# A limit of four on loaded rows of x, and a precedence of 0.1 on TensorE for the state streams, in a hybrid GLA and RWKV-7 step

## The chip, the cores and the metric

The kernel runs on one core of a Trainium2 chip. The metric is the device time of one execution in microseconds (us), as the median of several runs; lower is better. The profile is that of one execution.

## The reference, cut to what matters

One layer is computed for 1024 new tokens (the prompt) and 8 single tokens with a stored state each (the samples). All arithmetic is float32.

```python
p = x @ w_in                                  # (1024 + 8) x 1024 by 1024 x 9360 columns
p_gla, p_rwkv, p_gate = split(p)
o_gla, S_gla   = gated_linear_attention(p_gla)  # 4 heads, in chunks, silu-gated
o_rwkv, S_rwkv = rwkv7_scan(p_rwkv)             # 16 heads, one state of 64 x 64 each, silu-gated
m   = sigmoid(gate_a) * (o_gla @ w_up_gla) + sigmoid(gate_b) * (o_rwkv @ w_up_rwkv)
out = layernorm(2 ** 0.25 * x + m @ w_out)
# also returned: the final states S_gla and S_rwkv, and the last projected row, of prompt and samples
```

## The kernel before

**Tiling.** Everything is kept transposed: a row is a tile of 128 channels (partitions) by tokens. The tokens go in two passes (`PASS`, line 29): pass 0 has 512 prompt tokens and the 8 samples, in two column tiles of 260; pass 1 has the other 512 prompt tokens in one tile of 512. In each pass the 73 column groups of `w_in` are projected one after the other. One such projection is a block (`blocks`, line 670): for k from 0 to 7 three matmuls, `hi*xh`, `hi*xl` and `lo*xh`, since each float32 operand is split in a high and a low part. After both passes come the up-projections (of `o_gla`, then `o_rwkv`, pass 0, then pass 1) and the output projection (of `mg`, pass 0, then pass 1), also as blocks.

**The change of x.** Whenever the block stream goes on to another input, `load_x` (line 583) brings the eight row tiles of the new one: a DMA into a buffer of the pool `row` (`raws`), a copy on ScalarE into `xh{k}` (`high`, line 594; the finished ones stand in `his`), and a subtraction into `xl{k}` (`low`, line 602), which then frees the raw row. `xh{k}` and `xl{k}` exist once; they come free when the last block of the old input has done its step k (line 700). `load_x` is started three blocks ahead of that (`AHEAD`). There are eight changes: x of pass 0, x of pass 1, `o_gla` and `o_rwkv` of pass 0 and of pass 1, `mg` of pass 0 and of pass 1. For the two of x, `low_rank` (line 714) also multiplies the raw rows, in groups of three rows (0 to 2, 3 to 5, 6 and 7), into one PSUM bank of `big` for each column tile, and a raw row isn't freed before that.

**Buffers.** `row` has 26 buffers of 128 x 520 in SBUF. A block takes one row for its result before its first matmul, and, in both passes, only if another one is left over beside what is already waited for (`KEEP`, lines 268, 745, 1008, 1352). The eight PSUM banks are `proj` 2, `big` 3, `pch` 1, `pY` 2. `big` serves nearly all but the projections and the chain: the heads of GLA, `front`, `back`, `turn` and `norm` of the RWKV pairs.

**The streams.** For each of the 8 pairs of RWKV heads `pair` (line 1012) runs `front`, `back`, `turn`, `chain` and `norm`; `gla_head` (line 752) runs the four GLA heads, and in pass 0 `gla_sample` (line 886) after each of them, with eight rows held until line 863. At the end of a chain of pass 1, `state` (line 1219) takes a bank of `big`, transposes the final state `Sp` into it on TensorE, waits for the one buffer `sto`, copies, and frees the bank. `rwkv_sample` (line 1249) and `tails` (line 963) begin with transposes of the same sort; they run in one stream of the same kind, "state", from the second front of pass 1 on.

**The order.** All streams are Python generators, and a planner (`run`, line 357) puts their instructions in one order when the program is made. At each step it takes the operation with the smallest key: the start time that it estimates less a precedence, `ON_PE` for TensorE and `PRIO` for the others (line 365). Blocks have 0.0 on TensorE. A matmul with other array tiles than the one before counts as 0.09 later (`SWITCH`, lines 64 and 324); a transpose of `Sp`, 128 x 64, has other tiles than a block's 128 x 128. At equal keys the stream that stands first in the list wins. A stream that waits for a buffer offers no operation. Each engine then executes its instructions in exactly that order, and SyncE issues all DMAs in one queue in that order.

Of the kernel before, what the change touches and what calls it, by code (L numbers as in the profile page):

```python
# [55 lines left out]

KEEP = 1
AHEAD = 3
SPARE_ROWS = 8


# [12 lines left out]
PRIO = {"evacuate": 0.7, "pair": 0.4, "turn": 0.5, "chain": 0.5, "norm": 0.1, "x": 0.7, "lora": 0.2, "rank": -0.3,  # L74
        "head": 0.3, "gate": 0.05, "w": 0.3, "out": -0.1, "state": 0, "block": 0.0}
ON_PE = {"evacuate": 0.0, "pair": 0.15, "turn": 0.1, "chain": 0.15, "norm": 0.15, "x": 0.0, "lora": 0.15, "rank": 0.1,
         "head": 0.1, "gate": 0.06, "w": 0.0, "out": -0.03, "state": 0.0, "block": 0.0}

URGENT = 0.6
SIGMOID, EXP = "sigmoid_and_others", "natural_log_exp_and_others"  # L80
# [321 lines left out]
class Kern(Order):  # L402
# [180 lines left out]
    def load_x(self, src, i, wait=None, low_rank=False):  # L583

        if wait is not None:
            yield wait
        base, n = PASS[i][:2]
        raws, his, xs, used = [], [], [], [NK]
        self.xq.append(xs)
        if low_rank:  # L590
            used = [0]
            self.spawn(self.low_rank(self.ctx[i], raws, used), "rank")

        def high():
            for k in range(NK):
                yield lambda: len(raws) > k
                h = yield from self.get(f"xh{k}")
                yield self.A.copy(h[:, :n], raws[k])
                his.append(h[:, :n])

        def low():
            for k in range(NK):
                yield lambda: len(his) > k
                lo = yield from self.get(f"xl{k}")
                yield self.E.tensor_sub(lo[:, :n], raws[k], his[k].bitcast(F32))
                yield lambda: used[0] > k
                self.free(raws[k])
                xs.append((his[k], lo[:, :n]))
        self.spawn(high(), "x")
        self.spawn(low(), "x")  # L610
        for k in range(NK):
            raw = yield from self.row(n)
            rows = slice(k * P, (k + 1) * P)
            yield from self.load(f"x{k}", self.S.dma_start(
                raw, src[k] if isinstance(src, list) else src[rows, base:base + n]))
            raws.append(raw)
# [752 lines left out]
    def load_gates(self):  # L1369

        yield lambda: self.ctx[1].fronts == NPAIR and self.ctx[1].gated == NPAIR + 2 * GH
        for c in self.ctx:
            for n in range(2):
                for x in range(NK):
                    gt = yield from self.row(c.n, SPARE_ROWS)
                    yield self.S.dma_start(gt, self.sg[c.i][n][x])
                    m = None
                    if n:
                        m = yield from self.row(c.n, SPARE_ROWS)
                        yield lambda: c.half > x  # L1380
# [132 lines left out]
    def swap(self, src, i, wait=None, low_rank=False):  # L1513

        if self.plan:
            self.plan[-1].last = True
        self.todo = (max(0, len(self.plan) - AHEAD), (src, i, wait, low_rank))

# [135 lines left out]
```

## Time and profile before

| | us |
|---|---|
| median of 3 runs | 1686.61 (1685.98 to 1691.09) |
| the profiled execution | 1687.94 |
| its span, first to last instruction | 1686.2 |
| TensorE busy with matmuls in the span | 1628.7 |
| VectorE busy | 1184.6 |
| ScalarE busy | 830.7 |

Matmuls overlap, so a busy TensorE is one that has some matmul in it, at whatever clock. The granted clock is given as a share of 2.4 GHz; 0.50 is the lower of its two levels, 1.2 GHz. The page shows the span in 40 slices of 42 us, the windows show chosen stretches, the timeline single instructions with the idle time ahead of them and what ended it.

### The profile page before, as it was taken

The numbers are of one execution on the slowest core, as the hardware profiler recorded it, in microseconds if no ns is written. First come the engines' busy times: TensorE is split into PE (matmuls) and PEld (weight loads), VectorE is DVE, ScalarE is ACT, GpSimd is POOL, SyncE is SP. The second block draws the span as 40 slices with busy tenths as digits, with TensorE's granted clock in tenths as the row PEclk, the third lists the DMA queues.
The fourth block names the chain that finished last, engine by engine and source line by source line (L and its number), as shares of the span: only waits on it lengthen the run. The fifth ranks groups of instructions, "written<-read, shape, count | busy, mean of one in ns | idle before, by whom it ended". The sixth has DMA issues, their size and how long they took to land.

```text
span 1686.2 us, 29927 instructions
## 1 busy us (share of the span) xinstructions
PE 1628.7 (97%) x10322; PEld 1430.9 (85%) x10322; DVE 1184.6 (70%) x3114; ACT 830.7 (49%) x1974; POOL 86.0 (5%) x183
## 2 busy tenths in 40 slices
PE   8999999999999998999999999999989999999998
PEld 7899999999999996888878778778867889988786
DVE  6777876887688766757656477898728876656565
ACT  5456755664657465443634254526243656644210
POOL 1100000100000000000000000200000000000000
PEclk9999999999999999899999999999988999999999
DMA  9777675777587657545364625454642487788522
GB/s 291 246 228 231 217 215 152 227 246 218 160 245 228 216 158 237 170 119 174 101 206 123 186 73 176 152 163 156 202 145 67 114 275 221 236 278 278 182 78 87
DMA packets 311778, 315.26 MB, mean 187 GB/s; under 512 B 75347, under 2 KB 197084, under 8 KB 311628
## 3 DMA queue, kind: packets, MB, share of 16 engines
q1 hardware_dynamic: 311628, 313.36, 59.9%
q8 instruction: 82, 1.34, 0.3%
q14 instruction: 68, 0.56, 0.1%
HBM read 195.45 MB, written 117.82 MB: 186 GB/s over the span
## 4 chain that ended last, share of the span: by engine, by line
PE 73%; DVE 12%; DMA 7%; ACT 3%; issue 2%; SPq 2%; POOL 0%; POOLq 0%; DVEq 0%; ACTq 0%
PE proj L214 41%; PE big L214 21%; PE pY L214 7%; DVE row L214 4%; PE pch L214 4%; DMA wide<-LD 2%; SPq L214 2%; DVE X L214 2%; DVE Xt L214 2%; ACT row L214 1%; DVE wide L214 1%; DMA row<-state_rwkv 1%; DVE wlo L214 1%; DVE az L214 1%; DMA wraw<-w_up_gla 1%
## 5 line engine op out<-in xcount | busy, mean ns | idle before, releaser
L214 PE MATMUL proj<-xl,whi 128*128 128x260 f32 (+1 forms) x1928 | 637.5, 331 | 0.0
L214 PE MATMUL proj<-xh,whi 128*128 128x260 f32 (+1 forms) x1928 | 635.9, 330 | 0.0
L214 PE MATMUL proj<-xh,wlo 128*128 128x260 f32 (+1 forms) x1928 | 635.0, 329 | 0.0
L214 PEld LDWEIGHTS proj<-xh,wlo 128*128 128x128 f32 x1928 | 364.9, 189 | 29.9 <-issue 6.6
L214 PEld LDWEIGHTS proj<-xh,whi 128*128 128x128 f32 x1928 | 365.2, 189 | 28.5 <-issue 5.4
L214 PEld LDWEIGHTS proj<-xl,whi 128*128 128x128 f32 x1928 | 364.9, 189 | 28.6 <-issue 6.5
L214 DVE TENSOR_TENSOR row<-row 128x256 f32<-128x256 f32 (+6 forms) x326 | 161.7, 503 | 23.8 <-ACT row L214 11.8
L214 ACT CAST whi<-wraw 128x512 fp32r<-128x512 f32 x210 | 129.9, 622 | 95.7 <-PE proj L214 51.7
L214 DVE TENSOR_TENSOR wlo<-wraw,whi 128x512 fp32r<-128x512 f32 x205 | 141.0, 691 | 40.5 <-ACT whi L214 37.3
L214 ACT ACTIVATE row<-row 128x512 f32<-128x512 f32 (+4 forms) x229 | 138.4, 611 | 44.6 <-DVE row L214 26.3
L214 DVE TENSOR_TENSOR Xt<-X,wide 128x60 f32<-128x60 f32 (+24 forms) x496 | 105.4, 212 | 43.8 <-DMA wide<-LD 31.2
L214 ACT ACTIVATE row<-proj,omu 128x260 f32<-128x260 f32 (+1 forms) x99 | 54.1, 547 | 150.2 <-PE proj L214 149.9
L214 PE MATMUL big<-row 128*128 128x64 f32 (+4 forms) x712 | 115.6, 282 | 12.5 <-DVE row L214 11.5
L214 PEld LDWEIGHTS big<-row 128*128 128x128 f32 (+1 forms) x712 | 96.9, 193 | 23.3 <-DVE row L214 13.5
L214 ACT ACTIVATE s0p<-wide,pc 64x64 f32<-64x64 f32 x256 | 88.1, 344 | 52.7 <-DVE wide L214 48.5
L214 DVE TENSOR_TENSOR X<-X,Xt 128x60 f32<-128x60 f32 (+24 forms) x496 | 104.8, 211 | 11.9
L214 ACT COPY wide<-pch 64x64 f32<-64x64 f32 x221 | 45.5, 206 | 114.3 <-PE pch L214 110.4
L214 DVE SCALAR_TENSOR_TENSOR row<-proj,pv,row 128x259 f32<-128x259 f32 (+1 forms) x99 | 56.3, 569 | 49.7 <-ACT tail L214 33.7
L214 DVE SCALAR_TENSOR_TENSOR wide<-pch,pc,s0p 64x64 f32<-64x64 f32 x224 | 63.1, 282 | 38.3 <-PE pch L214 33.7
L214 POOL TENSOR_TENSOR row<-row 128x512 f32<-128x512 f32 (+7 forms) x43 | 45.5, 1059 | 794.4 <-ACT row L214 211.7
L214 ACT COPY row<-big 128x128 f32<-128x128 f32 (+7 forms) x165 | 46.7, 307 | 66.8 <-PE big L214 63.5
L381 ACT ACT_TABLE_LOAD x56 | 71.8, 1283 | 1.0
(254 smaller groups left out, 2560.6 us busy)
## 6 DMA issues: line engine op xcount, KB each, us to landing
wraw<-w_in SPq DMA_DIRECT2D x146, 256.0 KB
wh<-whi SPq DMA_DIRECT2D x146, 256.0 KB
wl<-wlo SPq DMA_DIRECT2D x146, 256.0 KB
whi<-wh SPq DMA_DIRECT2D x146, 256.0 KB
wlo<-wl SPq DMA_DIRECT2D x146, 256.0 KB
wide<-LD SPq DMA_DIRECT2D x64, 128.0 KB
wraw<-w_up_gla SPq DMA_DIRECT2D x32, 256.0 KB
wraw<-w_up_rwkv SPq DMA_DIRECT2D x32, 256.0 KB
```

Of the source, the lines that this page charges most:

```text
L214: ways.append((eng, lambda call=call: call(out, *args, **kw), price(eng, name, out, args, ins)))
L381: self.nc.scalar.preload_act_table_set(self.table)
```

## The change

Ahead of each raw row, `load_x` now waits until fewer than four rows are loaded and not yet copied into `xh`. The first change of x of the program is exempt: there `low_rank` is true and the pass, `i`, is 0. Streams of the kind "state" get the precedence 0.1 on TensorE in place of 0.0; on the other engines theirs stays 0.

```diff
+RAWS = 4
...
 ON_PE = {"evacuate": 0.0, "pair": 0.15, "turn": 0.1, "chain": 0.15, "norm": 0.15, "x": 0.0, "lora": 0.15, "rank": 0.1,
-         "head": 0.1, "gate": 0.06, "w": 0.0, "out": -0.03, "state": 0.0, "block": 0.0}
+         "head": 0.1, "gate": 0.06, "w": 0.0, "out": -0.03, "state": 0.1, "block": 0.0}
...
         self.spawn(high(), "x")
         self.spawn(low(), "x")
         for k in range(NK):
+            yield lambda: k - len(his) < RAWS or low_rank and not i
             raw = yield from self.row(n)
```

## Rows read from the trace of the kernel before

**Rows 1.** The page: busy time of the engines; granted clock by slices
```profile
PE 1628.7 (97%) x10322; PEld 1430.9 (85%) x10322; DVE 1184.6 (70%) x3114; ACT 830.7 (49%) x1974; POOL 86.0 (5%) x183
...
PEclk9999999999999999899999999999988999999999
```
**Rows 2.** Windows, long ones: from:to, length, TensorE busy (matmuls), clock, DMA share, GB/s
```profile
50.00:650.00 600.00, 590.39 (x4649) 1.00 0.69 213
700.00:1350.00 650.00, 627.60 (x3256) 0.98 0.48 145
1350.00:1686.00 336.00, 323.07 (x1860) 1.00 0.64 204
```
**Rows 3.** Windows of the stretches with a lower clock, same columns
```profile
672.00:680.00 8.00, 2.72 (x12) 0.54 0.47 160
680.00:688.00 8.00, 7.67 (x42) 0.61 0.10 35
960.00:996.00 36.00, 30.78 (x151) 0.86 0.26 76
1236.00:1280.00 44.00, 35.90 (x154) 0.77 0.20 62
```
**Rows 4.** Timeline of TensorE: start, us, instruction, idle before it and releaser
```profile
670.32 0.28 PE L214 MATMUL proj<-xl,whi 128*128 128x260 f32 x1
670.44 0.28 PE L214 MATMUL proj<-xh,wlo 128*128 128x260 f32 x1
676.22 1.02 PE L214 MATMUL big<-row 128*128 128x8 f32 x4 [5.49 <-DVE row L214]
...
680.68 1.02 PE L214 MATMUL big<-row 128*128 128x8 f32 x4 [0.33 <-DVE row L214]
681.56 0.57 PE L214 MATMUL proj<-xh,whi 128*128 128x260 f32 x1
```
**Rows 5.** Timeline of the DMA queue, first and last loads of x for pass 1 (eight in all)
```profile
646.30 1.43 SPq L214 DMA_DIRECT2D row<-xT  x2
...
654.82 0.65 SPq L214 DMA_DIRECT2D row<-xT  x1
```
**Rows 6.** Timeline of ScalarE, x of pass 1 is copied
```profile
693.41 4.27 ACT L214 CAST xh<-row 128x512 fp32r<-128x512 f32 x8
```
**Rows 7.** Timeline of VectorE, last writes of final states in chains of pass 1
```profile
846.60 0.60 DVE L214 SCALAR_TENSOR_TENSOR Sp<-pch,pc,s0p 64x64 f32<-64x64 f32 x2 [2.25 <-PE pch L214]
...
933.16 0.58 DVE L214 SCALAR_TENSOR_TENSOR Sp<-pch,pc,s0p 64x64 f32<-64x64 f32 x2
...
1018.51 0.58 DVE L214 SCALAR_TENSOR_TENSOR Sp<-pch,pc,s0p 64x64 f32<-64x64 f32 x2
...
1085.50 0.60 DVE L214 SCALAR_TENSOR_TENSOR Sp<-pch,pc,s0p 64x64 f32<-64x64 f32 x2 [0.19 <-PE pch L214]
...
1185.54 0.60 DVE L214 SCALAR_TENSOR_TENSOR Sp<-pch,pc,s0p 64x64 f32<-64x64 f32 x2 [0.31 <-PE pch L214]
```
**Rows 8.** Timeline of TensorE, transposes of final states and what follows them
```profile
962.32 0.27 PE L214 MATMUL big<-cons,smp 128*128 128x128 f32 x1
962.42 0.38 PE L214 MATMUL big<-cons,Sp 128*64 128x128 f32 x2
963.32 2.00 PE L214 MATMUL big<-X,gg 128*128 128x64 f32 x16 [0.52 <-ACT sto L214]
...
1237.96 0.49 PE L214 MATMUL big<-cons,Sp 128*64 128x128 f32 x3
```
**Rows 9.** The chain of work that ended last: a load of 256 KB, issue to use
```profile
671.00 3.68 DMA row<-vd
```
**Rows 10.** Timeline of VectorE, low parts of x for pass 1
```profile
694.07 4.90 DVE L214 TENSOR_TENSOR xl<-row,xh 128x512 fp32r<-128x512 f32 x8 [0.22 <-ACT xh L214]
```
**Rows 11.** Waits of TensorE after 1340 us: total, times, longest
```profile
PE big L214 <- DVE wlo L214: 1.0, 1, 1.0
PE pY L214 <- DVE xl L214: 0.6, 1, 0.6
```

## The prediction

> **What bounds the kernel now.** I read the page first. TensorE has matmuls in it for 97% of the span and its clock is full in all but three slices [rows 1]: the kernel is bound by TensorE, and only what empties it or slows its clock can be won. Second, the windows. From 50 to 650 us, nearly all of pass 0, 590.39 of 600 us are busy at a clock of 1.00, so 1.6% are idle; from 1350 us to the end it is as dense but for the last microseconds [rows 2]. From 700 to 1350 us, pass 1, busy time times clock is 627.60 x 0.98 = 615 of 650 us; at the 1.6% of pass 0 it would be 640. So about 25 us are lost in pass 1, beside what lies just ahead of it. Third, shorter windows around the low digits of the clock, which find three places: 672 to 688, 960 to 996 and 1236 to 1280 us [rows 3]. Busy time alone hides a part of them, since a matmul at 1.2 GHz is busy for twice as long; length less busy time times clock is the loss.
>
> Place A: 8 - 2.72 x 0.54 = 6.5 us and 8 - 7.67 x 0.61 = 3.3 us, and the idle time from 670.7 to 672, 1.3 us: 11.1 us. Place B: 36 - 30.78 x 0.86 = 9.5 us. Place C: 44 - 35.90 x 0.77 = 16.4 us [rows 3, 4]. Together 37.0 us, of which B and C are 25.9, the same as the 25 of the long window. Each value holds to about 1 us, as clock and busy share are means.
>
> **Why these places are there.** At A the timeline shows projections up to 670.44, then only the four groups of tiny products of `gla_sample`, the first after 5.49 us of waiting, and the next projection at 681.56, right behind the last of them [rows 4]. The projection has all its operands from pass 0; what it lacks can only be the row for its result. A count along the code at that point (no row of the trace shows the pool): GLA head 3 holds 8 rows, pair 7 holds 3, pair 6 in `norm` 3, gates 4, and x of pass 1 holds 8, since its loads are issued from 646.30 to 655.5 while the copies come only at 693.41 [rows 5, 6]. That is 26 of 26. The next rows to come free are those of head 3, behind its last tiny product, which is where the projection goes on.
>
> At B and C no x is loaded. There the banks of `big` run out. The final states of the first five pairs of pass 1 are written at 846.60, 933.16, 1018.51, 1085.50 and 1185.54 [rows 7]; their transposes, which hold a bank each from then on, run at 962.42 (two) and 1237.96 (three), 116, 29, 219, 152 and 52 us later [rows 7, 8]. In both cases the transposes stand directly ahead of the bubble, not after a wait for data. From the code: a block and a state both have 0.0, blocks always have a matmul ready, and a transpose of `Sp` pays 0.09 for the change of tiles, so the state never wins until the blocks stop. So from 933 to 962 us and from 1185 to 1238 us all three banks are taken (before 962 the third by the transpose of `smp`, which goes with the others [rows 8]), heads, fronts and norms stand still with their rows in hand, the rows run out, the blocks stop, and only then do the states go. Then the held-up work comes as one chain without projections between its links, which is the bubble.
>
> **The change, part by part.** *The limit.* It leaves four rows of x unloaded until `xh` comes free, so 22 of 26 rows are taken at A. The gate's temporary and the next block's row fit, and the two blocks left in pass 0 run there. A's 11.1 us go. The clock's part goes with it, since no pause is left to lower it. What is late next is the change of x itself, some 11 us earlier.
>
> What the limit adds is a wait at each of seven changes (the first is exempt): rows 4 to 7 are issued once a copy of rows 0 to 3 is emitted, and so behind more of the DMA queue, among the weight loads and the stores of gates; the queue holds nothing back by it, for the wait is in the planner and no instruction of SyncE waits for a copy. TensorE's bound from below is nothing, or a little less than nothing (four loads fewer compete with the weights): what hides the load is the rest of the old input's last block, 7 steps, and the new one's first four. Matmuls of 260 columns start 0.12 us apart [rows 4], so a step of three takes 0.36 us and 11 steps 3.9 us; with 512 columns they take longer. The bound from above is a whole load, copy and subtraction: 3.68 us [rows 9], 4.27/8 = 0.5 us [rows 6] and 4.90/8 = 0.6 us [rows 10], 4.8 us for each change, 33.6 us for seven. The values now, with all rows there, are waits of 1.0 and 0.6 us near such changes [rows 11]. I take 0.7 us each, by these rows and by 3.9 of 4.8 us being covered: 5 us in all. The low-rank products of the last five rows of x move behind the copies; their sum stays, and they fill the wait there. Their bank is held from the start of the load to the change as before.
>
> Against holding loads back there is a rule. The Trainium skill, "Trainium Kernel Development and Optimization", section Best Practices, tells to double-buffer so that DMA overlaps compute. By it each late load would show whole, which is the rival "late x" below; the trace has it both ways, as the early rows are what takes the buffers at A.
>
> *The precedence.* With 0.1 a state transpose has a key of +0.09 - 0.1 = -0.01 against a block, and wins; the one of `smp` wins by 0.1. No instruction is added; eight transposes of `Sp` and a few others, 0.1 us from start to start [rows 8], change places. Waits that they bring: at most the copy and the store behind one `sto`, and the states are 67 us or more apart [rows 7]. The bank comes back within a few us, B and C have three banks, as pass 0 has, and pass 0 has no such bubble. B and C give 25.9 us; at pass 0's 1.6%, the 60 us of dense work that stays in A, B and C keeps 1.0 us idle. `rwkv_sample` starts about 100 us earlier and holds its three to five rows earlier; between 996 and 1236 us it held them with no loss of that size, so I cost it at nothing, and at one more place like A, 11 us, if that cover is gone.
>
> *Sum.* 37.0 - 1.0 - 5 = 31 us. The profiled execution took 1687.9 us, 1.3 us over the median of the runs; 1686.6 - 31 = 1655.6, so 1656 us. Nothing behind pass 1 takes the gain back: the last chains would be done earlier too, as they wait for banks in C, and from 1350 us on TensorE is full [rows 2].
>
> **The rivals.** *Only A (0.17).* The margin of 0.01 lies inside estimates: other streams change the tiles too, a state's start may be estimated 0.01 later, and then the second part doesn't do what it says; or rows, not banks, are what B and C lack. For it: rows were short at A with a bank free. Against: the transposes start each bubble. Time: 1686.6 - 11.1 + 5 = 1680.5, without the late loads 1675.5.
>
> *Only B and C (0.08).* The blocks stop near 670 us for want of something else, or the stop moves a block further: 1686.6 - 24.9 + 5 = 1667.
>
> *Late x (0.07), slower.* Every change shows the whole load, 33.6 us, and TensorE stands long enough that its clock falls as at A, where the 8 us behind the pause lost 3.3 us [rows 3], 23.1 us in all. With the 36 us gained at A, B and C this is 1686.6 + 56.7 - 36 = 1707. It decides from 36/7 = 5.1 us a change, against a bound of 4.8 without the clock. Against: the cover of 3.9 us or more just worked out.
>
> *Nothing moves (0.04).* All bubbles return elsewhere, since another buffer is short: 1687.
>
> **How the numbers follow.** Forecast 0.64, 1656 us, its own range 1646 (late loads cost nothing, 36 us gained, and some 4 us of the other 10 us lost in pass 1 besides) to 1667 (one new place like A). The range takes in "only A" as well: 1645 to 1682. Left out are late x, nothing moves and a tail of the forecast, under 0.2. Bound for "the same": 0.3%, about what a measurement tells, 5 us, so 1681.5 to 1691.7. Faster: 0.64 + 0.08 + most of only A, 0.13, is 0.85; the same: 0.04 + 0.04 = 0.08; slower: 0.07.
>
> **What would show it.** Right: no stretch of projections ends without another near 670 us; loads of x for pass 1 come in two lots, the second with the copies; each transpose of `Sp` starts within some 5 us of its last write, the first near 840 us, and not two or three in a row; the clock is full throughout pass 1; busy time times clock from 700 to 1300 us is at 98% or more. Wrong: transposes of `Sp` still in groups (then only A); a wait for `xl` or `xh` of over 2 us at most changes of x (then late x); a bubble with tiny products and no projections elsewhere, say where the sample's step takes its rows.

## The result, and the profile after

| | before | after |
|---|---|---|
| median of the runs, us | 1687.66 (1685.98 to 1691.09, 4 runs) | 1659.75 (1656.93 to 1662.12, 4 runs) |
| the profiled execution, us | 1687.94 | 1659.17 |
| its span, us | 1686.2 | 1657.4 |

The ratio is 0.983, 95% interval 0.981 to 0.985: 28 us less, where 31 were forecast, and 1659.75 us where 1656 stood.

The page of the changed kernel: busy times, and the granted clock in its 40 slices.

```profile
PE 1618.6 (98%) x10322; PEld 1420.0 (86%) x10322; DVE 1181.6 (71%) x3106; ACT 836.6 (50%) x1986; POOL 82.2 (5%) x179
...
PEclk9999999999999999999999999999999999999999
```

As many matmuls as before [rows 1], 10 us less of busy time, and no slice with a low clock. Windows (from:to, length, TensorE, its weight loads, VectorE, ScalarE, GpSimd, clock, DMA share, GB/s):

```profile
672.00:680.00 8.00, 7.85 (x59) 6.65 (x58) 7.31 (x26) 5.22 (x10) 1.36 (x1) 1.00 0.83 271
680.00:688.00 8.00, 8.00 (x35) 3.87 (x35) 7.00 (x20) 3.56 (x8) 0.00 (x0) 1.00 0.89 291
700.00:1300.00 600.00, 590.73 (x3166) 488.23 (x3165) 430.12 (x1216) 280.40 (x687) 32.02 (x66) 1.00 0.50 152
1350.00:1656.00 306.00, 296.94 (x1702) 257.63 (x1700) 181.04 (x345) 112.22 (x219) 2.77 (x3) 0.99 0.62 198
```

Place A, with 2.72 and 7.67 us busy at half the clock before [rows 3], is full. Pass 1 is busy for 98.5% at full clock, just over the 98% named as the sign, and as dense as pass 0 was [rows 2]; B and C are gone. Next the loads of x for pass 1 in the DMA queue (start, us), and the copies of x and of `o_gla` on ScalarE:

```profile
647.40 1.46 SPq L216 DMA_DIRECT2D row<-xT  x2
652.15 0.96 SPq L216 DMA_DIRECT2D row<-xT  x2
...
676.33 4.47 SPq L216 DMA_DIRECT2D row<-xT  x4
```
```profile
678.42 1.66 ACT L216 CAST xh<-row 128x512 fp32r<-128x512 f32 x3 [0.45 <-PE proj L216]
...
1335.51 1.68 ACT L216 CAST xh<-row 128x520 fp32r<-128x520 f32 x3
1337.61 0.62 ACT L216 CAST xh<-row 128x520 fp32r<-128x520 f32 x1
1341.71 0.62 ACT L216 CAST xh<-row 128x520 fp32r<-128x520 f32 x1 [0.86 <-DMA row<-o_gla]
```

Two lots in place of one [rows 5], and the copy of x comes 15.0 us earlier than at 693.41 [rows 6]. The copies of `o_gla` now wait for their second lot; that is the late x of the forecast. The transposes of final states on TensorE (start, us; first three and last of `Sp`, and one of `smp`):

```profile
832.77 0.27 PE L216 MATMUL big<-cons,smp 128*128 128x128 f32 x1
...
839.59 0.27 PE L216 MATMUL big<-cons,Sp 128*64 128x128 f32 x1
...
926.70 0.30 PE L216 MATMUL big<-cons,Sp 128*64 128x128 f32 x1
...
1004.19 0.27 PE L216 MATMUL big<-cons,Sp 128*64 128x128 f32 x1
...
1426.75 0.27 PE L216 MATMUL big<-cons,Sp 128*64 128x128 f32 x1
```

Each of the eight runs alone, 0.7 to 1.0 us behind the last write of its state (838.64, 926.05, 1003.24 and so on to 1425.87 us), where before a bank stayed taken for up to 219 us [rows 7, 8].

**Where the time came from.** The first copies of x of pass 1 and of `o_gla` of pass 0 cut the span in three:

| stretch, us | before | after | less by |
|---|---|---|---|
| start to the copy of x of pass 1 | 693.4 | 678.4 | 15.0 |
| from there to the copy of `o_gla` (pass 1) | 671.5 | 657.1 | 14.4 |
| from there to the end | 321.3 | 321.9 | -0.6 |

The stretches don't hold quite the same work. The groups of matmuls by form show what crossed the cuts. Ten low-rank products, 12 tiny products of `gla_sample` and 4 of 260 columns moved from the first stretch to the second. The ten, and what one pair of them takes up to the next projection, 0.96 us:

```profile
L216 PE MATMUL big<-row,wa x10: 592/598/603, 679.0 to 688.2; 128*16 128x512 f32 x10
```
```profile
682.89 1.03 PE L216 MATMUL big<-row,wa 128*16 128x512 f32 x2
683.85 0.50 PE L216 MATMUL proj<-xh,wlo 128*128 128x512 f32 x1
```

That is 10 x 0.48 + 12 x 0.09 + 4 x 0.13 = 6.4 us. From the third stretch to the second came 4 products of 512 columns (0.46 us each), 14 of 128 (0.11) and three transposes, 3.7 us. Like for like the second stretch gained 14.4 + 6.4 + 3.7 = 24.5 us, and the third lost 0.6 + 3.7 = 4.3.

Most of what the third stretch loses lies at the change to `o_gla` of pass 0. A load in the chain that ended last (start, then us from issue to use), and a window of TensorE (busy, clock, DMA share, GB/s):

```profile
1339.21 6.04 DMA row<-o_gla
```
```profile
1335.00:1350.00 15.00, 12.05 (x60) 0.89 1.03 296
```

The last late rows take 6.04 us, where the forecast took 3.68 [rows 9]. TensorE waits five times for `xh` and `xl` (2.9 us in all, the longest 1.18), and from 1346 to 1348 us it has the lower clock. That makes 15 - 12.05 x 0.89 = 4.3 us of loss; before, the 15 us from 1364 on, at the same change, lost 15 - 13.99 = 1.0 us at full clock.

### The profile page after: what moved, and what is told of

Read it like the earlier page. It is cut to its first block, busy times and chain, and to the rows that moved or that the text cites. A ratio compares the mean times of both kernels' runs of the same rounds, so it can differ in the third digit from the quotient of the medians.

```text
span 1657.4 us, 29919 instructions
## 1 busy us (share of the span) xinstructions
PE 1618.6 (98%) x10322; PEld 1420.0 (86%) x10322; DVE 1181.6 (71%) x3106; ACT 836.6 (50%) x1986; POOL 82.2 (5%) x179
## 4 chain that ended last, share of the span: by engine, by line
PE 74%; DVE 13%; DMA 6%; SPq 3%; ACT 2%; issue 2%; POOL 0%; POOLq 0%; DVEq 0%; ACTq 0%
PE proj L216 39%; PE big L216 23%; PE pY L216 7%; DVE row L216 4%; PE pch L216 4%; SPq L216 3%; DMA wide<-LD 3%; DVE X L216 2%; DVE Xt L216 2%; DVE wide L216 2%; ACT row L216 1%; DVE wlo L216 1%; DVE pair L216 1%; DMA row<-o_gla 1%; DMA LD<-gg 1%
## 5 line engine op out<-in xcount | busy, mean ns | idle before, releaser
L216 PE MATMUL proj<-xl,whi 128*128 128x260 f32 (+1 forms) x1880 | 620.9, 330 | 0.0
L216 PE MATMUL proj<-xh,whi 128*128 128x260 f32 (+1 forms) x1880 | 618.6, 329 | 0.0
L216 PE MATMUL proj<-xh,wlo 128*128 128x260 f32 (+1 forms) x1880 | 617.8, 329 | 0.0
L216 PEld LDWEIGHTS proj<-xh,wlo 128*128 128x128 f32 x1880 | 355.0, 189 | 29.0 <-issue 6.5
L216 PEld LDWEIGHTS proj<-xh,whi 128*128 128x128 f32 x1880 | 355.3, 189 | 26.3 <-issue 4.8
L216 PEld LDWEIGHTS proj<-xl,whi 128*128 128x128 f32 x1880 | 355.1, 189 | 25.9 <-issue 4.9
L216 DVE TENSOR_TENSOR row<-row 128x512 f32<-128x512 f32 (+8 forms) x333 | 162.1, 495 | 18.5 <-ACT row L216 7.9
L216 ACT COPY wide<-pch 64x64 f32<-64x64 f32 x224 | 46.2, 206 | 102.3 <-PE pch L216 98.6
L216 POOL TENSOR_TENSOR row<-row 128x512 f32<-128x512 f32 (+5 forms) x36 | 39.5, 1098 | 763.6 <-ACT row L216 347.4
L216 ACT COPY row<-big 128x128 f32<-128x128 f32 (+8 forms) x165 | 46.8, 307 | 52.3 <-PE big L216 47.2
```

The source lines that it names most:

```text
L216: ways.append((eng, lambda call=call: call(out, *args, **kw), price(eng, name, out, args, ins)))
```

## The experiments

Times are medians; the kernel before had 1687 us beside each group (1686.99, 1687.28 and 1687.61). Stretches are cut as in the table above.

**One part alone.** The limit without the precedence:

```diff
-         "head": 0.1, "gate": 0.06, "w": 0.0, "out": -0.03, "state": 0.1, "block": 0.0}
+         "head": 0.1, "gate": 0.06, "w": 0.0, "out": -0.03, "state": 0.0, "block": 0.0}
```

> The limit without the precedence. Theory: place A is a shortage of rows, B and C one of banks, and the two parts of the change act apart. A's 11 us go, B and C stay: 1687 - 11 = 1676 us (1673 to 1680). The trace should show the clock full from 668 to 690 us, x of pass 1 copied near 680 us, and transposes of Sp in groups of two and three with a bubble behind each, some 12 us earlier than before. Rival, rows are what lacks at B and C too and the limit relieves them: the whole gain, 1660 us, with no bubble in pass 1.

1680.64 us (1674.79 to 1685.27, ten runs), ratio 0.996, 0.995 to 0.998: a gain of 6 us, 0.6 us outside what I gave. Windows of A and of the old places B and C, 10 us earlier (here and below: TensorE busy, clock, DMA share, GB/s), and the transposes of `Sp`:

```profile
672.00:680.00 8.00, 7.89 (x62) 1.00 0.86 270
680.00:688.00 8.00, 8.00 (x35) 1.00 0.88 306
950.00:986.00 36.00, 30.77 (x157) 0.91 0.31 98
1226.00:1270.00 44.00, 35.82 (x161) 0.81 0.19 62
```
```profile
953.42 0.38 PE L216 MATMUL big<-cons,Sp 128*64 128x128 f32 x2
...
1227.57 0.49 PE L216 MATMUL big<-cons,Sp 128*64 128x128 f32 x3
```

A is full. B and C still lose 36 - 30.77 x 0.91 = 8.0 and 44 - 35.82 x 0.81 = 15.0 us (9.5 and 16.4 before), behind a group of two and one of three as in [rows 8]. The limit doesn't relieve them, so this rival falls. The run doesn't tell whether rows lack there for another reason, since no x is loaded at B and C; the two experiments on margin and holding below decide that.

The precedence without the limit:

```diff
-            yield lambda: k - len(his) < RAWS or low_rank and not i
```

> The precedence without the limit. Theory: B and C go, A stays with its pause of 5.5 us, its tiny products alone from 676 to 681 us and its low clock: 1687 - (29 - 11) = 1669 us (1665 to 1672). Rival, the bubbles of pass 1 are set off by the pause at A, which puts the streams out of step: then they stay, 1680 us or more. Rival, B and C are worth the 25.9 us that length less busy time times clock gave: 1661 us.

1668.29 us (1667.4 to 1670.57), ratio 0.989, 0.986 to 0.992. The same windows, and one more between them:

```profile
672.00:680.00 8.00, 2.29 (x10) 0.68 0.52 172
680.00:688.00 8.00, 7.67 (x46) 0.68 0.10 35
880.00:890.00 10.00, 7.72 (x25) 0.66 0.52 162
950.00:986.00 36.00, 35.14 (x230) 1.00 0.49 145
1226.00:1270.00 44.00, 41.84 (x221) 1.00 0.48 142
```

A stands as before, B and C are gone. So the two parts act nearly apart: by the medians they gain 6 and 19 us, 25 of the 28 us of both. From 880 to 890 us 10 - 7.72 x 0.66 = 4.9 us are lost behind one wait of 2.51 us for `l2p`, an operand of `front`; with them pass 1 would have gained 15.0 + 3.7 + 4.9 = 23.6 us like for like, nearly the 24.5 of the change.

**Margin or holding.** The precedence at 0.08, under the 0.09 of a change of array tiles:

```diff
-         "head": 0.1, "gate": 0.06, "w": 0.0, "out": -0.03, "state": 0.1, "block": 0.0}
+         "head": 0.1, "gate": 0.06, "w": 0.0, "out": -0.03, "state": 0.08, "block": 0.0}
```

> The change with a precedence of 0.08 in place of 0.1, just under the 0.09 that a change of array tiles costs. Theory: the margin decides, a transpose of Sp still loses to blocks that are ready, but one of smp, with the tiles of a block, wins and gives its bank back. Then banks are short later than before and stay so: transposes of Sp more than 20 us after their last write, again with bubbles, 1665 to 1677 us. Rival, any precedence does, since other streams change the tiles often enough: each transpose within 5 us of its last write, 1660 us.

1674.89 us (1669.62 to 1676.06). Those of `smp` run at 831.42 and 833.08, as early as in the change; those of `Sp` wait in twos again, the first of each pair over 100 us (last writes at 837.28, 923.66, 1014.35 and 1083.54):

```profile
958.14 0.38 PE L216 MATMUL big<-cons,Sp 128*64 128x128 f32 x2
...
1124.03 0.41 PE L216 MATMUL big<-cons,Sp 128*64 128x128 f32 x2
```

Around these two pairs TensorE loses 36 - 28.98 x 0.95 = 8.5 us from 955 us on and 40 - 36.22 x 0.91 = 7.0 us from 1120 us on. In these traces pass 1 takes 674.6 us, like the 674.3 of the limit alone, whose trace is its fastest run; by the medians 0.08 gains 6 of the 21 us between the limit alone and the change. The 0.01 that the forecast stood on is real, and carries most of the second part.

Then the other way round: the precedence stays, but a state takes its bank, and so runs, only when all fronts of pass 1 have begun.

```diff
     def state(self, p, S):
+        yield lambda: self.ctx[1].fronts == NPAIR
         pt = yield from self.bank("big", [C, P])
```

> The change, with each state stream made to wait, before it takes its bank, until all eight fronts of pass 1 have begun; the transposes then come in one group near 1320 us. Theory: a held bank is the cause of B and C, not a transpose that comes late, so nothing is lost: 1660 us (1657 to 1663). Rival, it is the early transposes that help, by what waits for their results: the losses of B and C come back, 1672 to 1680 us.

1663.63 us (1659.07 to 1666.94), ratio 0.986, 0.982 to 0.989: 0.6 us over what the theory gave, far below the rival. The trace separates them too: six transposes run from 1320.43 to 1326.19 us, and pass 1 loses nothing (656.1 us against 657.1):

```profile
1320.43 0.27 PE L216 MATMUL big<-cons,Sp 128*64 128x128 f32 x1
...
1326.19 0.30 PE L216 MATMUL big<-cons,Sp 128*64 128x128 f32 x1 [0.31 <-ACT sto L216]
1342.26 0.30 PE L216 MATMUL big<-cons,Sp 128*64 128x128 f32 x1 [1.36 <-ACT sto L216]
```

Nobody waits for an early transpose; what hurt was the bank taken long before it. The late ones queue behind the one `sto`, and the last stretch has 323.2 us in place of 321.9, a difference too small to be read.

**What the limit costs, and where.** The limit at the change to x of pass 1 alone:

```diff
-            yield lambda: k - len(his) < RAWS or low_rank and not i
+            yield lambda: k - len(his) < RAWS or not (low_rank and i)
```

> The change, with the limit only at the change to x of pass 1, so that the six later changes load all eight rows ahead as before. Theory: the limit costs a few us there, at most the 4 to 5 us that the stretch behind pass 1 lost beside what it was relieved of: that stretch, from the first copy of o_gla to the end, falls from 321.9 us to 317 to 320 us, the start and pass 1 stay as in the change (678 and 657 us), 1656 to 1659 us in all. Rival, late x costs nothing and the loss there has another cause: 1660 us, with 321 to 323 us in that stretch. Rival, the early rows fill the pool again at the change to o_gla and hold blocks up: over 1663 us.

1666.95 us (1662.29 to 1667.48), ratio 0.987, 0.985 to 0.990. Start and pass 1 are as in the change (678.4 and 658.2), but the last stretch takes 328.9 us, 7 more: my theory had the wrong sign, and the third rival has the time. Two parts of it take 4.9 us more each, from the first copy of `o_gla` to that of `o_rwkv` (68.9 against 64.0) and from `mg` of pass 0 to `mg` of pass 1 (60.3 against 55.4); the parts between give 2.6 back. The first loss, in the DMA queue, on TensorE and in a window:

```profile
1376.36 4.22 SPq L216 DMA_DIRECT2D row<-o_rwkv  x8
```
```profile
1378.81 2.00 PE L216 MATMUL big<-X,gg 128*128 128x64 f32 x16 [1.73 <-DVE X L216]
...
1389.76 0.79 PE L216 MATMUL pch<-wide,gg 128*128 128x128 f32 x2 [2.00 <-ACT wide L216]
```
```profile
1376.00:1394.00 18.00, 13.74 (x74) 0.66 0.80 246
```

The eight rows of `o_rwkv` are loaded while the last pair of pass 1 still runs, and its chain goes nearly without blocks at half the clock: the picture of A, 18 - 13.74 x 0.66 = 8.9 us. That the pool is empty there is argued from A, not seen, and early rows alone don't bring this loss: with the precedence alone the eight are loaded from 1385.10 us on, also while the last pair runs, and from 1350 to 1411 us TensorE is busy for 58.19 of 61 us at full clock. What else it takes stays open. The second loss is at the change to `mg`, where the kernel before had it too (its DMA queue and TensorE first, then the queue of the change):

```profile
1577.90 3.77 SPq L214 DMA_DIRECT2D row<-mg  x8
...
1583.27 0.37 SPq L214 DMA_DIRECT2D row<-w_out  x1
```
```profile
1587.80 0.49 PE L214 MATMUL proj<-whi,xh 128*128 128x512 f32 x1 [2.25 <-ACT whi L214]
```
```profile
1547.04 0.43 SPq L216 DMA_DIRECT2D row<-w_out  x1
1551.64 1.89 SPq L216 DMA_DIRECT2D row<-mg  x4
```

The last load of `w_out`, which also takes a row, stood behind eight loads of `mg`, and TensorE waited 2.25 us for its copy (2.99 in this experiment). With the limit it goes ahead of the rows for pass 1.

Two rows (`RAWS = 2` in place of 4), three (3), five (5), six (6) and seven (7):

> The change with two rows in place of four. Theory: what hides a late load is the work of the steps before it; rows 2 to 7 now come two by two, each pair a load, a copy and a subtraction (4.8 us) behind the one before, 14 us for the last, against a cover of 4 us with 260 columns and some 8 with 512: 6 to 10 us of waiting at each of seven changes where it shows in full, less where other matmuls fill it. I expect waits for xl and xh of over 2 us at most changes and 1675 to 1710 us. Rival, other streams fill all of it, so that a late load costs nothing here: 1660 us.

> The change with three rows in place of four. The last rows now come one load, copy and subtraction (4.8 us) later than with four, less what the steps hide: 2 to 5 us more at most changes, 1668 to 1690 us, between the 1660 us of four rows and the 1710 us of two. Rival, the cover is used up only below three: 1660 us.

> The change with five rows in place of four. By the count 23 of 26 rows are taken at A, which is enough: x of pass 1 copied at 678 to 681 us. Late rows are three in place of four, so no more waiting for them: 1656 to 1662 us. Rival, as with six rows: a place at the change to o_gla, where the late rows were issued 5 us behind the first copy, and bubbles in pass 1: 1668 us or more.

> The change with six rows in place of four. By the count 24 of 26 rows are taken at A: one block gets its row, the second of the two left does not. The pause comes one block later, and is shorter: copies from 682 to 689 us, 1661 to 1667 us. Rival, two free rows are enough, as one block gives its row back before the next wants one: near 679 us, 1660 us. Rival, the same as seven rows: 690 us or later.

> The change with seven rows in place of four. Theory by the count of the pool: 18 rows are held beside those of x, so 25 of 26 are taken, a block wants one and another left over, and place A comes back whole: x of pass 1 copied from 690 to 694 us, TensorE at a low clock from 672 to 688 us, 1667 to 1672 us. Rival, one row is all that the blocks lacked: copied near 679 us, 1660 us.

All, with four (as measured first) and with no limit (the precedence alone):

| rows | time, us | copy of x of pass 1 | pass 1 | first copy of `o_gla` to that of `o_rwkv` | rest |
|---|---|---|---|---|---|
| 2 | 1709.88 | 675.4 | 663.2 | 84.3 | 280.7 |
| 3 | 1681.60 | 678.4 | 665.9 | 78.9 | 255.2 |
| 4 | 1659.75 | 678.4 | 657.1 | 64.0 | 257.9 |
| 5 | 1655.39 | 679.5 | 656.8 | 63.0 | 255.5 |
| 6 (one run) | 1679.91 | 689.0 | 664.6 | 67.8 | 256.7 |
| 7 (one run) | 1672.89 | 692.7 | 656.8 | 63.8 | 257.8 |
| none | 1668.29 | 693.2 | 656.5 | 61.2 | 257.9 |

The copy of x bears out the count of the pool row by row: up to 23 of 26 taken A is gone, with 24 it stands one block later (projections run to 676.6 us in place of 670.4), with 25 it is whole. The times came out less well: five rows are 0.6 us below the range that I gave, seven 0.9 us above it and six 13 us above it, the last two by one run each. At the other end late x costs what its rival feared: with two rows the kernel is slower than before, ratio 1.014, 1.011 to 1.016, and TensorE waits 16.6 + 12.0 + 1.9 us for `xh` behind 1300 us:

```profile
PE pY L216 <- ACT xh L216: 16.6, 7, 8.1
PE big L216 <- ACT xh L216: 12.0, 5, 6.6
...
PE proj L216 <- ACT xh L216: 1.9, 3, 0.9
```

A round of load and copy there took 11.8, 5.1 and 4.8 us (copies of `o_gla` at 1338.56, 1350.32, 1355.43 and 1360.25); the later two are the 4.8 us that the forecast took as its bound, the first is well over. Six rows, the slowest of those above three, shows one reason. ScalarE, the DMA queue and TensorE:

```profile
1357.30 0.62 ACT L216 CAST xh<-row 128x520 fp32r<-128x520 f32 x1
1364.71 1.27 ACT L216 CAST xh<-row 128x520 fp32r<-128x520 f32 x2
```
```profile
1356.01 2.25 SPq L216 DMA_DIRECT2D az<-ln  x3
1358.30 0.43 SPq L216 DMA_DIRECT2D row<-w_out  x1
1358.78 1.17 SPq L216 DMA_DIRECT2D row<-o_gla  x2
```
```profile
1365.39 0.59 PE L216 MATMUL pY<-xh,whi 128*128 128x260 f32 x1 [5.22 <-ACT xh L216]
```

The two rows left over are issued 5.2 us behind the first copy (1353.62), after loads of `ln` and of `w_out`; they then take 5.91 us to their use, and TensorE stands for 5.22 us. So what stands ahead of a late row in SyncE's queue can cost more than the number of late rows: six rows have two late ones and 67.8 us in this stretch, four rows have four and 64.0. Below four rows the number tells too (78.9 and 84.3 us). Pass 1, too, takes 6 to 9 us longer with two, three and six rows; with three and six, TensorE waits 2.97 us (at 871) and 2.76 us (at 876) for `X`, written by VectorE in `front`. Why the new order brought these waits stays open.

Last, no limit at the change to `o_gla` of pass 0, and the change itself beside it:

```diff
-            yield lambda: k - len(his) < RAWS or low_rank and not i
+            yield lambda: k - len(his) < RAWS or not i and (low_rank or src is self.o_gla)
```

> The change, with no limit at the change to o_gla of pass 0. Theory: the late rows of o_gla cost 5 us in the stretch up to the first copy of o_rwkv (64.0 us in the change against 62.4 before, though 3.7 us of work left it), and the early rows take no buffer there that others lack. That stretch falls to 58 to 61 us, the rest stays: 1654 to 1657 us. Rival, the rows are what the gates and the weights of w_out lack, as in the kernel that limits the first change alone: no gain or a loss, 1660 to 1666 us.

> The changed kernel itself, beside the other three of this group: 1657 to 1662 us, as before.

The change again: 1660.74 us (1656.35 to 1664.23), ratio 0.984, 0.981 to 0.986. With the exemption: 1656.68 (1653.28 to 1664.34), ratio 0.983, 0.980 to 0.986, not told apart in time. Its stretch from `o_gla` to `o_rwkv` takes 59.4 us in place of 64.0, as the theory had it, and TensorE is busy for 14.18 of the 15 us from 1332 us on, at full clock: late x costs about 5 us at that one change. Five rows, in the same group, have the lowest median: 1655.39 (1652.84 to 1656.92), ratio 0.981, 0.979 to 0.983; the intervals of four and five rows overlap.

## Why the prediction was right, point by point

| term, us | forecast | measured |
|---|---|---|
| place A | 11.1 | 9.6 |
| places B and C, less the idle time that stays | 24.9 | 24.5 |
| late x | -5 | -7.5 |
| from `mg` of pass 0 to `mg` of pass 1 | 0 | 3.2 |
| start of pass 0 | 0 | -1.0 |
| sum | 31 | 28.8 |

- **A.** The stretch is 15.0 us shorter, of which 6.4 are work moved behind the cut; the same low-rank pair already starts 1.0 us later at 652 us (652.23 against 651.22), before the change can act. 15.0 - 6.4 + 1.0 = 9.6. The forecast had said that low-rank products move behind the copies, but not the tiny ones with them. The cause is shown by the number of rows at which A comes back.
- **B and C.** Length less busy time times clock was the right price: 24.5 of 24.9 us. The cause is shown from both sides: transposes that still wait keep the loss (0.08), late ones that hold no bank don't bring it.
- **Late x** came near its total by luck. I took 0.7 us at each of seven changes, 5 in all. The parts of the last stretch, with its 3.7 us, say 5.3 us at `o_gla` of pass 0, 1.1 and 1.2 at the next two and nothing after, 7.5 in all. At x of pass 1 hardly anything is seen: TensorE is busy for 15.85 of the 16 us from 672 to 688 us. The part from `mg` to `mg` gains 3.2 us that I had at nothing, because the early rows there were in the way of `w_out`; so the stretch as a whole lost 4.3. The mis-sized term is the late load at `o_gla`: a cover of 3.9 us was to hide a load of 3.68, but the load took 6.04 there, and the clock fell behind the waits, which I had only in the rival.
- "Nothing behind pass 1 takes the gain back" came true, but the last stretch isn't safe by itself: with the limit at one change only it takes 7 us more.
- **The rivals' prices.** Only A was put at 1680.5 and measures 1680.6, closer than ten runs that spread over 10 us can bear out; only B and C at 1667, measured 1668.3. Late x was put at 1707 for four rows, which no run shows; two rows measure 1709.9, some 50/7 = 7 us a change over four rows, where the rival began at 5.1. Four rows lie two steps from that edge.
- These terms come from one execution on each side, and the change's own traces differ by up to 2.8 us in a part of the last stretch (43.4 and 46.2 us): terms that differ by less than 2 or 3 us say nothing.

The Trainium skill, "Perfetto Trace Analysis", section Optimization Strategy, says that the same gap, repeating on the engine that should be full, can mean too little SBUF or PSUM for the next tile. The runs agree on the cause, rows (SBUF) at A and banks (PSUM) at B and C, though these are three places and not one gap that repeats. No buffer had to be added: 4 of 26 rows were held by loads that weren't due, and up to three banks by transposes that could have run. The rule to double-buffer (the Trainium skill, "Trainium Kernel Development and Optimization", section Best Practices) holds here up to five rows ahead, 1709.88 us with two and 1655.39 with five; the eight rows of a full copy ahead cost 13 us against five (1668.29).

## What to carry to other kernels

When a full engine shows bubbles, find out which pool is empty there, and which of its buffers are held by work that could run at once or needn't have been loaded yet; price the bubble as length less busy time times clock. A limit on loading ahead has two edges, so measure a few values, look at what stands ahead of the late load in its queue, and take the time of a load from a stretch as full as the one where it will come (6.04 us here, not 3.68). A precedence must beat the scheduler's own penalties: 0.08 gave 6 of the 21 us that 0.1 gave.

## What was not expected of the hardware

- Executions of one program differ along with their mean granted clock. Ten of the limit alone span 1673.0 us at 0.992 up to 1683.5 at 0.988; five with no limit at `o_gla` span 1651.2 us at 0.998 up to 1662.6 at 0.992. Bubbles alone don't set the spread: four of the precedence alone, which keeps the one at A, span 1665.6 to 1668.7. What sets it stays open. The trace of the limit alone is its fastest run, which is why it shows 13 us of gain (1686.2 - 1673.0) where the median shows 6.
- The load of a row of about 256 KB took 3.68 us from issue to use at one place [rows 9], where the DMA engines' share was 0.47 (672 to 680 us), and 6.04 us at another, where it was 1.03. In other runs the load at that other place took from 4.65 us (precedence 0.08) to 5.91 (six rows), 7.00 (the change again) and 7.02 (three rows).
- One wait of 2.51 us on TensorE was followed by a fall to half the clock (0.66 from 880 to 890 us, with the precedence alone); it cost 4.9 us. The kernel before waited 2.17 us at the same instruction, and its clock stayed at 1.00 (878 to 888 us), as did the change's at waits of 1.44 us (913 to 923 us) and 1.27 us (1230 to 1240 us). At `o_gla` the change's clock fell behind five waits of at most 1.18 us each.
